# Strided heads' values of two head pairs by Strassen's seven half-size products, spread over the chunks of q and k

## The chip, the core and the metric

The kernel runs on one core of one Trainium2 chip. The time is device microseconds of one execution, as the median of several runs. A profiled execution has a span, from its first to its last instruction, and a trace from which all rows below come. The engines are TensorE (PE; PEld is its weight load), VectorE (DVE), ScalarE (ACT), GpSimd (POOL) and SyncE (SP), which here only issues DMAs, as POOL mostly does.

## The reference, cut to what matters

Two layers of a decoder trunk on x of 512 tokens by 1024 features. Layer 0 is attention with 24 heads in three groups of eight (window and dilation 128 and 1, 512 and 4, 2048 and 16), layer 1 a gated recurrence; each is followed by a gated FFN with a short convolution, and each half layer sits between two RMS norms. The part that changes is the attention:

```python
qkv = (x @ w_qkv).reshape(B, S, N_GROUPS, 3, HEADS_PER_GROUP, HEAD_DIM)
for g in range(N_GROUPS):
    o, lse = dilated_group_attention(qkv[:, :, g, 0], qkv[:, :, g, 1], qkv[:, :, g, 2],
                                     tbl, WINDOWS[g], DILATIONS[g])
    ...
alpha = jax.nn.softmax(jnp.stack(lses), axis=0)
o = jnp.sum(alpha[..., None] * jnp.stack(outs), axis=0)
return o.reshape(B, S, ATTN_OUT_WIDTH).astype(x.dtype) @ w_o
```

The values of the two dilated groups, `qkv[:, :, 1, 2]` and `qkv[:, :, 2, 2]`, are plain products of the normed x (512 x 1024) with weights (1024 x 2048 in all).

## The kernel before

**Products.** Every large product is made in three passes (`PASSES`, L250): both operands are split into hi and lo parts in fp32r, and hi*hi, hi*lo and lo*hi are added in PSUM. `hT` is the normed x, transposed, as such a pair, [128, 8, 512]: features on the partitions, eight chunks k of 128 features, 512 tokens. A product of 512 columns over eight chunks takes 24 matmuls and fills one of eight PSUM banks.

**Weights.** `plan` lists the weight loads in the order of use, 1 MB each. `load` (L188) puts a DMA on SP's queue into one of three `raw` buffers; `pump` (L165) cuts a raw into two pieces and splits each, two ScalarE copies (hi) and two VectorE subtracts (lo) of 512 columns, into one of eight units (`W_UNITS`). `take` hands a unit to a product, `done` gives it back. All program text is in one hand-written order, and each engine works through its own part of it in that order.

**Ticks.** After each tile of 24 matmuls `tick` (L221) is called. It advances the side work (generators in `sides`, each with a delay in ticks), and pumps one piece, or two if fewer than six units are live. So softmaxes, transposes and weight splits come between the tiles of the large products.

**Attention.** First the local group: per pair of heads (`hp`) a chunk of q and a chunk of k (`feat_tiles`, two tiles each; q is evicted by ScalarE, k by VectorE), and for every second pair `values` for four heads. `local` then makes scores S, softmax, transposes PT and output O of one head and leaves the output `o0` in SBUF. Then the two dilated groups together: per pair four chunks (q and k of either group), then `values` (L605): for each of four tiles of 128 tokens 24 matmuls, with `hT` as the stationary and the weights as the moving operand; the tile goes to DRAM (`vrows`) and returns regrouped by residue (`vp`, `by_residue`). `strided` (L719) handles one head: S for both groups and the softmax with the local group's share at its first step, transposes PT two ticks later, O four ticks after that. The tiles of `values` lie between S and PT, and for the last pair they are the last large product ahead of the output projection.

**Output projection.** `rows_proj` (L401) multiplies the heads' outputs, split by `prep` into A[k] (hi and lo), with w_o, in an order of (token tiles, chunks of two heads), here `SHORT_ORDER` (L40). Heads 6 and 7 are chunk 3. When a token tile has all its chunks, `norms` adds it to x and makes the next `hT`. x stays in SBUF (`x_sb`) throughout; gains are loaded to two buffers.

Of the kernel before, what the change touches and what calls it, by code (L numbers as in the profile page):

```python
# [18 lines left out]
P = 128  # L19
S = 512  # L20
# [21 lines left out]
]  # L42

# [34 lines left out]
def kernel(  # L78
# [59 lines left out]
    x_sb = cp.tile([P, 4, D], F32, tag="x_sb", name="x_sb")  # L138

    def gain(src, layer, eng=nc.gpsimd):  # L140
        g = cp.tile([P, D], F32, tag="gain", name=nm("gain"), bufs=2)
        row = src[layer]
        eng.dma_start(g, bass.AP(tensor=row.tensor, offset=row.offset, ap=[[0, P], [1, D]]))
        return g
# [9 lines left out]

    def parts_of(kind, raw):

        if kind == "feat":
            return [raw[:, :, m * P : (m + 1) * P] for m in range(2)]
        if kind == "value":
            return [raw[:, 2 * i : 2 * i + 2, :] for i in range(2)]  # L160
        if kind == "rows":
            return [raw[:, i : i + 1, :] for i in range(2)]
        return [raw]

    def pump(limit=2):  # L165

        for _ in range(limit):
            i = state["cv"]
            if not pieces and i < state["dma"]:
                pieces.extend((i, j, u) for j, u in enumerate(parts_of(plan[i][0], raws.pop(i))))  # L170
                state["cv"] += 1
            if pieces and state["live"] < W_UNITS:
                i, j, raw = pieces.pop(0)
                hi, lo = (
# [12 lines left out]

    def load():  # L188
        i = state["dma"]
        kind, kd, cols, srcs = plan[i]  # L190
        raw = wp.tile([P, kd, cols], F32, tag="raw", name=nm("raw"), bufs=RAW_BUFS)
        at = 0
        for src, n in srcs:
            if i < 2:
                for k in (0, 2):
                    nc.sync.dma_start(raw[:, k : k + 2, :], src[:, k : k + 2, :])
            else:
                nc.sync.dma_start(raw[:, :, at : at + n] if kind == "value" else raw[:, at : at + n, :], src)
            at += n
        raws[i] = raw  # L200
        state["dma"] += 1
# [44 lines left out]

    def w_rows(w, r0):
# [38 lines left out]
    def prenorm(t, hT, g, wait):  # L286
        xh, gh = halves(x_sb[:, t, :]), halves(g)
# [22 lines left out]
    def first_norm(tiles, g):  # L310
# [5 lines left out]
        for j, t in enumerate(tiles):  # L316
            for i, h in enumerate(halves(x_sb[:, t, :])):
# [19 lines left out]
        for j, t in enumerate(tiles):  # L337
            for i, h in enumerate(halves(x_sb[:, t, :])):
# [5 lines left out]
    def postnorm(t, banks, g, final):  # L344
        xh, gh = halves(x_sb[:, t, :]), halves(g)
# [55 lines left out]
    def rows_proj(nchunks, act, order, post, pre):  # L401
# [6 lines left out]
        def prep(n):  # L408
            for k in seq[:n]:
                if k not in A:  # L410
                    A[k] = act(k)
# [6 lines left out]
    def rows_run(nchunks, A, prep, seq, order, post, pre):  # L418
        post_g = gain(*post)
        pre_g, hT = (gain(*pre), new_hT()) if pre is not None else (None, None)  # L420
# [39 lines left out]
    def act_split(srcs):  # L460
        def f(k):
            hi, lo = gen(F32R, "ahi"), gen(F32R, "alo")
# [91 lines left out]
    def attention(hT, post, pre):  # L554
# [50 lines left out]
        def values(vs, permute, midway=None):  # L605

            if permute:
                vd = dp.tile([S, 512], F32, name=f"vrows{len(vrows)}")
                vrows.append(vd)
# [3 lines left out]
            for t in range(4):  # L613
# [22 lines left out]
                for u in (0, 1) if begin and t == 1 else (t,):  # L636
                    o = gen(s="v")
                    nc.scalar.activation(o, banks[u], AF.Copy)
                    if permute:
                        nc.sync.dma_start(vd[u * P : (u + 1) * P, :], o)  # L640
                    else:
                        vs.append(o)
                if t == 3 and permute:
                    by_residue(vd, vs)
                if midway and t == 1:
                    midway()
                tick()

# [21 lines left out]
        def local(h, hh, q, k, v):  # L670
# [46 lines left out]
            o0.append(o)  # L717

        def strided(h, hh, qks, v):  # L719
            st1 = st1_box[0]  # L720
            mx = small(12)
            Ls = []
            for gi, (q, k) in enumerate(qks):
# [10 lines left out]
                Ls.append(L)  # L734
            M, nM, c0, den, s12 = small(4), small(4), small(4), small(4), small(8)
# [44 lines left out]
            o3 = o0[h].rearrange("p (a c) -> p a c", a=4)  # L780
            nc.vector.tensor_tensor(o3, o3, cn.unsqueeze(2).to_broadcast([P, 4, P]), op=ALU.mult)
            yield 4
# [6 lines left out]
            for a in range(4):  # L789
                c = slice(a * P, (a + 1) * P)  # L790
                nc.tensor.transpose(pt0[:, c], o0[h][:, c], ident)
# [24 lines left out]
        next(build)  # L816
        for hp in range(4):
            q, k = [], []
            if hp % 2 == 0:
                v = []  # L820
                values(v, False)
# [3 lines left out]
            feat_tiles(2, hT, qk_sink(q, k, False))  # L825
# [3 lines left out]
        prep, run = rows_proj(4, act_split(oT), SHORT_ORDER, post, pre)  # L829
        for hp in range(4):  # L830
            qs, ks, v = [], [], []
            feat_tiles(4, hT, qk_sink(qs, ks, True))
            both = [(qs[2 * g : 2 * g + 2], ks[2 * g : 2 * g + 2]) for g in range(2)]
            for hh in range(2):
                side(strided(2 * hp + hh, hh, both, v), 1 + hh)
            last = hp == 3
            values(v, True, (lambda: prep(2)) if last else None)
            if last:
                prep(4)
        return run()  # L840
# [97 lines left out]
    qkv, w_in = attn_w_qkv[0], lru_w_in[0]  # L938
    for hp in range(4):
        if hp % 2 == 0:  # L940
            w_value(qkv, (2 * D + hp * 256, 512))
        for j in range(2):
            w_cols(qkv, j * D + hp * 256)
    for hp in range(4):
        for g, j in ((1, 0), (1, 1), (2, 0), (2, 1)):
            w_cols(qkv, g * 3 * D + j * D + hp * 256)
        w_value(qkv, *((g * 3 * D + 2 * D + hp * 256, 256) for g in (1, 2)))
# [28 lines left out]
    for i in range(2):  # L976
        c = slice(i * 512, (i + 1) * 512)
        nc.sync.dma_start(x_sb[:, 0, c], x[0, 0:P, c])
    g = gain(norm_mix_pre, 0, nc.sync)
    load()  # L980
    for t in range(1, 4):
        nc.sync.dma_start(x_sb[:, t, :], x[0, t * P : (t + 1) * P, :])
# [58 lines left out]
```

## Time and profile before

| | |
|---|---|
| median of 3 runs | 1493.47 us (1491.96 to 1495.49) |
| span of the profiled execution | 1492.5 us |
| mean granted TensorE clock | 0.996 |
| stretch 460 to 520 us: TensorE busy | 59.06 of 60.00 us |
| HBM read, over the span | 150.14 MB |

The time of the profiled execution is shown by its span only; the median of the runs stands 1.0 us above it. Values of the strided heads lie at 229.5 us and three times after it, the last ending near 484 us, where the first matmul of the output projection starts (484.1 us). A group row reads: line, engine, operation, output<-inputs, partitions x elements, count | busy us, mean ns of one | idle us before them and who ended it. A timeline row reads: start, duration, engine, line, operation, count of merged instructions, and in brackets the idle time before it. A wait row reads: who waited <- for whom: us in total, times, longest.

### The profile page before, as it was taken

The page shows a single profiled execution, that of the slowest core. Times are in us where ns is not written, and L with a number is a line of the kernel's source. Part 1 is how long each engine was busy: PE and PEld are TensorE (multiplying, and loading weights), DVE is VectorE, ACT ScalarE, POOL GpSimd, SP SyncE. Part 2 cuts the span into 40 slices and gives each one's busy share as a digit, 9 for nine tenths or more (in the row PEclk, how much of TensorE's full clock was granted, in tenths as well). Part 3 has the DMA queues.
Part 4 walks back from the last instruction along what each step waited for, and adds up shares of the span by engine and source line. Part 5 has one row for each costly group of instructions (what it writes and reads, how often), then busy time and mean ns, then how long its engine had stood idle before and what let it go on. Part 6 is the DMA issues. An engine that isn't in the chain of part 4 may idle for free.

```text
span 1492.5 us, 18131 instructions
## 1 busy us (share of the span) xinstructions
PE 1477.9 (99%) x7097; PEld 1240.6 (83%) x7097; DVE 792.7 (53%) x1611; ACT 630.9 (42%) x1282; POOL 34.1 (2%) x67
## 2 busy tenths in 40 slices
PE   8999999999999999999999999999999999999998
PEld 6788888888888898888888888988798888888886
DVE  6344334343434676555565336877876555565333
ACT  5333334343334554344344334479554334344321
POOL 0130000000000000000000000000000000000000
PEclk9999999999999999999999999999999999999999
DMA  7543122424243324232233231342233332323301
GB/s 229 200 140 122 64 88 93 141 92 141 92 141 113 113 93 138 86 104 94 86 112 114 87 111 43 101 145 81 85 99 113 96 102 89 110 85 115 111 1 57
DMA packets 116278, 157.66 MB, mean 106 GB/s; under 512 B 5135, under 2 KB 97511, under 8 KB 116192
## 3 DMA queue, kind: packets, MB, share of 16 engines
q1 hardware_dynamic: 111296, 145.24, 29.3%
q0 software_dynamic: 4896, 11.26, 2.3%
q8 instruction: 56, 0.92, 0.3%
q14 instruction: 30, 0.25, 0.0%
HBM read 150.14 MB, written 11.05 MB: 108 GB/s over the span
## 4 chain that ended last, share of the span: by engine, by line
PE 88%; ACT 5%; DVE 4%; DMA 2%; issue 1%; SPq 0%; POOL 0%; DVEq 0%; ACTq 0%; POOLq 0%
PE ps L254 52%; PE acc L254 22%; PE v L623 8%; DVE wlo L148 1%; DVE xb L853 1%; ACT whi L147 1%; PE S L729 1%; PE tr L303 1%; PE O L787 1%; PE O L714 1%; DMA raw<-in_attn_w_qkv_dram 1%; DMA toe<-skew 1%; ACT sig L874 1%; PE S L679 1%; PE PT L768 0%
## 5 line engine op out<-in xcount | busy, mean ns | idle before, releaser
L254 PE MATMUL ps<-hT,whi 128*128 128x512 f32 (+1 forms) x2752 | 802.1, 376 | 0.0
L254 PEld LDWEIGHTS ps<-hT,whi 128*128 128x128 f32 x2752 | 502.9, 188 | 92.6 <-ACT qk L600 0.6
L254 PE MATMUL ps<-hT,wlo 128*128 128x512 f32 (+1 forms) x1376 | 515.2, 374 | 0.0
L148 DVE TENSOR_TENSOR wlo<-raw,whi 128x512 fp32r<-128x512 f32 x504 | 322.8, 686 | 272.0 <-ACT whi L147 271.8
L147 ACT ACTIVATE whi<-raw 128x512 fp32r<-128x512 f32 x504 | 285.3, 623 | 141.1 <-PE acc L254 120.9
L254 PEld LDWEIGHTS ps<-hT,wlo 128*128 128x128 f32 x1376 | 259.0, 188 | 46.5
L527 DVE SCALAR_TENSOR_TENSOR u<-ps,cols,u 128x511 f32<-128x511 f32 x192 | 143.8, 749 | 140.6 <-ACT u L523 137.2
L254 PE MATMUL acc<-whi,alo 128*128 128x512 f32 x512 | 199.4, 389 | 1.0 <-DVE alo L148 1.0
L254 PE MATMUL acc<-whi,ahi 128*128 128x512 f32 x512 | 200.0, 391 | 0.0
L254 PE MATMUL acc<-wlo,ahi 128*128 128x512 f32 x512 | 199.2, 389 | 0.0
L523 ACT ACTIVATE u<-ps,cols 128x512 f32<-128x512 f32 x96 | 74.8, 779 | 210.1 <-PE ps L254 210.1
L623 PE MATMUL v<-whi,hT 128*128 128x512 f32 x384 | 125.2, 400 | 0.9 <-ACT hT L307 0.9
L254 PEld LDWEIGHTS acc<-whi,alo 128*128 128x128 f32 x512 | 96.1, 188 | 21.4 <-DVE alo L148 1.4
L254 PEld LDWEIGHTS acc<-whi,ahi 128*128 128x128 f32 x512 | 96.1, 188 | 19.7
L254 PEld LDWEIGHTS acc<-wlo,ahi 128*128 128x128 f32 x512 | 96.1, 188 | 19.6
L623 PEld LDWEIGHTS v<-whi,hT 128*128 128x128 f32 x384 | 73.0, 191 | 16.8 <-ACT hT L307 1.6
L623 PE MATMUL v<-wlo,hT 128*128 128x512 f32 x192 | 75.2, 395 | 0.0
L538 ACT ACTIVATE u<-u 128x512 f32<-128x512 f32 x48 | 30.3, 632 | 80.4 <-DVE u L527 80.4
L666 DVE CUSTOM_DVE_ANT_0 L<-S,toe 128x128 f32<-128x128 f32 (+1 forms) x96 | 25.2, 320 | 52.9 <-DMA toe<-skew 22.2
L600 ACT ACTIVATE qk<-ps 128x512 f32<-128x512 f32 x24 | 14.3, 596 | 88.7 <-PE ps L254 76.9
L602 DVE COPY qk<-ps 128x512 f32<-128x512 f32 x24 | 16.6, 691 | 63.0 <-PE ps L254 63.0
L349 DVE TENSOR_TENSOR post<-acc,gain 128x512 f32<-128x512 f32 x32 | 21.8, 687 | 45.7 <-ACT junk L261 45.7
(166 smaller groups left out, 914.9 us busy)
## 6 DMA issues: line engine op xcount, KB each, us to landing
raw<-in_ffn_w_up_dram SPq DMA_DIRECT2D x48, 1024.0 KB, 5.2
raw<-in_attn_w_qkv_dram SPq DMA_DIRECT2D x26, 1024.0 KB, 5.0
raw<-in_ffn_w_down_dram SPq DMA_DIRECT2D x24, 1024.0 KB, 5.0
raw<-in_attn_w_qkv_dram SPq DMA_DIRECT2D x20, 512.0 KB, 5.6
raw<-in_lru_w_in_dram SPq DMA_DIRECT2D x8, 1024.0 KB, 5.4
skew<-rowv POOLq DMA_DIRECT2D x3, 1536.0 KB, 12.2
vrows<-v SPq DMA_DIRECT2D x16, 256.0 KB, 2.5
vp<-vrows SPq DMA_DIRECT2D x16, 256.0 KB, 3.8
```

The lines of the kernel that those rows point to most:

```text
L147: nc.scalar.activation(hi, raw, AF.Copy)
L148: nc.vector.tensor_tensor(lo, raw, hi.bitcast(F32), op=ALU.subtract)
L254: mm(dst, l[a], r[b], start=start and n == 0, stop=stop and n == 2)
L303: nc.tensor.transpose(ps[:, k * P : (k + 1) * P], xs[i][:, k * P : (k + 1) * P], ident)
L349: nc.vector.tensor_tensor(u[i], banks[i], gh[i], op=ALU.mult)
L523: nc.scalar.activation(u, ps, AF.Identity, scale=cc[:, j : j + 1], bias=cc[:, 48 + j : 49 + j])
L527: nc.vector.scalar_tensor_tensor(u[:, d:], ps[:, : S - d], wc, u[:, d:], op0=ALU.mult, op1=ALU.add)
L538: nc.scalar.activation(u, u, AF.Gelu_apprx_tanh)
L602: nc.vector.tensor_copy(dst, src)
L623: mm(banks[t], hT[a][:, k, t * P : (t + 1) * P], W[b][:, k % 2, :], start=(k, a, b) == (0, 0, 0), stop=(k, a, b) == (KD - 1, 1, 0),)
L666: nc.vector.tensor_tensor_reduce(dst, ps, bias, scale=1.0, scalar=3 * NEG, op0=ALU.add, op1=ALU.max, accum_out=mx)
L679: mm(Sp[a // 2][:, o + lo : o + 256], q[hh][:, a * P : (a + 1) * P], k[hh][:, k0 : (a + 1) * P], start=True, stop=True)
```

## The change

The strided heads' values of two head pairs are made together: two pairs of 512 columns side by side, tokens cut into two halves of 256, features into two halves of 512, so that a product of 2 x 2 by 2 x 2 blocks results. Seven block products (in the Winograd form, with sums of hT and of the weights) take the place of eight. Each product is 256 tokens by 512 columns over four chunks of k, in two PSUM banks. The seven are six steps (the first has two products); the first block's steps stand behind the q and k chunks of local pairs 1 to 3, the second's behind the chunks of strided pairs 0 and 1 named in `VALUE_STEPS`. Sums of weights are made in `added`, from raws that are loaded again where needed; sums of hT by `make`, as side work, into buffers that held x; x is loaded again at the end. Local heads' outputs go to DRAM and back (`ow`). Strided pair 3 has no values behind it: its heads score group 1 ahead of the last two chunks, and the output projection takes `LAST_ORDER`. The lru stage keeps `SHORT_ORDER`.

```diff
+LAST_ORDER = [
+    ([0, 1], [0, 1, 2]), ([2], [0]), ([0], [3]), ([1], [3]), ([3], [0]), ([2, 3], [1]), ([2], [2, 3]), ([3], [2, 3]),
+]
+VALUE_STEPS = [(0, 1), (0, 2), (0, 3), (1, 0), (1, 1), (1, 2)]
...
+    def added(kind, j, raw):
+        if kind == "sum0" and j == 0:
+            total["sum"] = cp.tile([P, 4, 512], F32, tag="gain", name=nm("sum"))
+        h = slice(2 * j, 2 * j + 2)
+        part = total["sum"][:, h, :]
+        for n in range(2):
+            old = total["held"][:, h, :] if kind == "sum0" else part
+            nc.vector.tensor_tensor(part[:, n, :], old[:, n, :], raw[:, n, :], op=ALU.add)
+        return part
...
+            terms_of = {
+                3: [((1, 1), 1), ((0, 1), -1)],
+                2: [((0, 0), 1)],
+                4: [((1, 0), -1)],
+                1: [((0, 1), 1), ((0, 0), -1)],
+            }
+            def make(*names):
+                for name in names:
+                    terms = terms_of[name]
+                    T = tuple(cp.tile([P, 4, 256], F32R, tag="x", name=nm("T"), bufs=4) for _ in range(2))
+                    made[name] = T
+                    for m in range(2):
+                        r = run[m].rearrange("p (k c) -> p k c", k=2)
+                        h = slice(2 * m, 2 * m + 2)
+                        parts = [(cut(*ij, x)[:, h, :].bitcast(F32), sg) for ij, sg in terms for x in range(2)]
+                        if name in (3, 1):
+                            (a, _), (b, _) = parts[:2]
+                            nc.vector.tensor_tensor(r, a, b, op=ALU.add)
+                            parts = parts[2:]
+                        for a, sg in parts:
+                            nc.vector.tensor_tensor(r, r, a, op=ALU.add if sg > 0 else ALU.subtract)
+                        split(T[0][:, h, :], T[1][:, h, :], r)
+                        yield 1
...
+        def product(banks, act):
+            i = chunk()
+            for j in range(2):
+                W = take(i, j)
+                for u in range(2):
+                    for k in range(2):
+                        for n, (a, b) in enumerate(PASSES):
+                            mm(
+                                banks[u],
+                                act(a)[:, 2 * j + k, u * P : (u + 1) * P],
+                                W[b][:, k, :],
...
+                done()
...
+            def steps():
+                q = two()
+                c = [gen(s="c") for _ in range(2)]
+                product(q, block(0, 0))
+                for u in range(2):
+                    nc.scalar.activation(c[u], q[u], AF.Copy)
+                q = two()
+                product(q, block(1, 0))
+                o = [gen(s="v") for _ in range(2)]
+                each(o, c, q, ALU.add)
+                out(0, 0, o)
+                side(make(3, 2))
+                yield
+                chunk()
+                q = two()
+                y = [gen(s="y") for _ in range(2)]
+                product(q, total_of(3))
+                each(y, c, q, ALU.add)
+                side(make(4))
+                yield
+                q = two()
+                product(q, total_of(2))
+                each(y, q, y, ALU.subtract)
+                each(c, q, c, ALU.subtract)
+                side(make(1))
+                yield
...
-            o0.append(o)
+            od = dp.tile([P, 512], F32, name=f"o0d{h}")
+            nc.sync.dma_start(od, o)
+            o0.append(od)
...
+                if ahead and not gi:
+                    yield 1
...
-            yield 4
+            yield 2 if ahead else 4
...
         for hp in range(4):
             qs, ks, v = [], [], []
-            feat_tiles(4, hT, qk_sink(qs, ks, True))
...
+            for j in range(4):
+                if j == 3:
+                    by_residue(vrows[hp], v)
+                if j == 2 and last:
+                    both = [(qs[:2], ks[:2])]
+                    heads = [strided(6 + hh, hh, both, v, True) for hh in range(2)]
+                    for g in heads:
+                        next(g)
+                feat_tiles(1, hT, lambda m, ps: sink(2 * j + m, ps))
+                if (hp, j) in VALUE_STEPS:
+                    step(j)
             if last:
+                both.append((qs[2:], ks[2:]))
                 prep(4)
+                for hh, g in enumerate(heads):
+                    next(g)
+                    side(g, 3 + hh)
+                for t in range(4):
+                    xs_sb[t] = load_x(t)
...
+    def quarters(p0):
+        def q(kind, i, f):
+            return kind, qkv, i, [(g * 3 * D + 2 * D + (p0 + f) * 256, 256) for g in (1, 2)]
+        return [
+            [q("value", 0, 0), q("value", 1, 0)],
+            [q("held", 0, 0), q("sum0", 0, 1)],
+            [q("sum", 1, 1)],
+            [q("sum", 1, 0)],
+            [q("value", 1, 1)],
+            [q("held", 0, 1), q("sum0", 1, 1)],
+        ]
```

The remaining steps 3 to 5 make the products of block (1, 1), of sum 4 and of sum 1 in the same manner: one changes c, one writes two tiles out, the last changes y and c and writes both.

More of the change, by code (lines that the diff above doesn't have):

```diff
@@ L173, in pump @@
                 i, j, raw = pieces.pop(0)
+                if plan[i][0] in ("sum0", "sum"):
+                    raw = added(plan[i][0], j, raw)
                 hi, lo = (
@@ L603, in qk, with values @@
             return o
[L605 to L609, printed above, removed]
+        def values(vs):
             ids = [chunk(), chunk()]
@@ L816, in attention, with step @@
         next(build)
+        def step(n):
+            next(steps)
+            tick()
         for hp in range(4):
@@ L975 @@
     root_table()
[L976 to L979, printed above, removed]
+    xs_sb.append(load_x(0, 2))
+    g = gains((norm_mix_pre, 0), eng=nc.sync)[0]
     load()
     for t in range(1, 4):
[L982 removed]
+        xs_sb.append(load_x(t))
         if t == 1:
```

153 lines of the change are left out of this document (115 added, 38 removed).

## The prediction

> **What bounds the kernel now.** First the page's totals and its chain of work, then the list of waits of TensorE alone.
>
> ```profile
> span 1492.5 us, 18131 instructions
> ...
> PE 1477.9 (99%) x7097; PEld 1240.6 (83%) x7097; DVE 792.7 (53%) x1611; ACT 630.9 (42%) x1282; POOL 34.1 (2%) x67
> ...
> PE 88%; ACT 5%; DVE 4%; DMA 2%; issue 1%; SPq 0%; POOL 0%; DVEq 0%; ACTq 0%; POOLq 0%
> ```
>
> ```profile
> PE acc L254 <- DVE alo L148: 1.0, 1, 1.0
> PE O L787 <- DMA vp<-vrows: 0.9, 1, 0.9
> ...
> PE O L714 <- DVE PT L706: 0.5, 1, 0.5
> ```
>
> TensorE is busy 99% and makes 88% of the chain. Once the values have begun it waits three times in the whole attention, 2.4 us in all. The stage lasts as long as its TensorE instructions, and what another engine does is free until TensorE waits for it. How much room the others have is in the busy times by stretch (stretch, length; PE, PEld, DVE, ACT, POOL; clock, DMA share, GB/s), local heads first, then strided ones:
>
> ```profile
> 62.00:170.00 108.00, 107.51 (x525) 88.83 (x524) 41.33 (x128) 39.52 (x99) 17.21 (x31) 1.00 0.38 126
> ...
> 345.00:460.00 115.00, 115.00 (x575) 97.39 (x574) 42.72 (x112) 37.75 (x90) 2.14 (x4) 1.00 0.33 112
> ```
>
> VectorE is busy 0.38 of either. I price the matmuls removed, then VectorE's new work, then the places where it reaches TensorE.
>
> **What is removed.** The page's groups of the values, and TensorE's timeline around one tile of them:
>
> ```profile
> L623 PE MATMUL v<-whi,hT 128*128 128x512 f32 x384 | 125.2, 400 | 0.9 <-ACT hT L307 0.9
> ...
> L623 PE MATMUL v<-wlo,hT 128*128 128x512 f32 x192 | 75.2, 395 | 0.0
> ```
>
> ```profile
> 380.91 0.39 PE L623 MATMUL v<-whi,hT 128*128 128x512 f32 x1
> ...
> 386.35 1.95 PE L729 MATMUL S<-qk,qk 128*128 128x128 f32 x16
> ```
>
> 576 matmuls are six calls of `values` with 96 each; four are the strided ones. Two of these (192) become seven products of 24 (two banks, four chunks of k, three passes), 168; twice over, 48 matmuls go. One tile of 24 takes 386.35 - 380.91 = 5.44 us, 0.227 each (the means of 400 overlap). Gain: 48 x 0.227 = **10.9 us**. I call 5.44 us a slot: a product or a tile of q or k fills one.
>
> Two of the three waits go too: `vp` is fetched a chunk of q and k earlier (0.9), and ([2], [0]) now lies between the last head and the use of its output (1.0): **1.9 us**.
>
> **VectorE's new work.** Prices, from its timeline, from the page for a PSUM source, and from a split that follows directly on an add (VectorE and ScalarE):
>
> ```profile
> 409.74 2.50 DVE L148 TENSOR_TENSOR wlo<-raw,whi 128x512 fp32r<-128x512 f32 x4
> ```
>
> ```profile
> L349 DVE TENSOR_TENSOR post<-acc,gain 128x512 f32<-128x512 f32 x32 | 21.8, 687 | 45.7 <-ACT junk L261 45.7
> ```
>
> ```profile
> 502.61 1.47 DVE L148 TENSOR_TENSOR alo<-oT,ahi 128x512 fp32r<-128x512 f32 x2
> ```
>
> ```profile
> 502.72 0.63 ACT L147 ACTIVATE ahi<-oT 128x512 fp32r<-128x512 f32 x1 [0.33 <-DVE oT L794]
> ```
>
> Back to back, 512 columns take 0.61 us (0.69 alone, and as much from PSUM). A block of two pairs adds: sums of the activations, 2 halves x (3+2+2+3 adds + 4 splits) = 28; sums of the weights, 4 x 4 = 16; splits of 28 half pieces in place of 16, 12; combinations of the products, 16. That is 72 x 0.61 = 44 us, 88 for both blocks; ScalarE gets 8 + 12 and loses 6 of 8 evictions, 14 x 0.6 = 8 us a block. Each block runs over some 145 us of TensorE (local: 6 chunks 65, products 38, values 22, heads 22), which held about 0.38 x 145 = 55 us of VectorE. 99 of 145 fits on average, so most of it costs nothing; it costs where it bunches, since VectorE takes its work in program order and TensorE's small products wait at its end. A half of a sum with three adds takes 3 x 0.61 + 0.70 for ScalarE's copy + 0.65 = 3.2 us, with two 2.6. A piece of weights takes 1.2, a summed one 2.4.
>
> *Place 1, heads 2 and 3.* Two rows of VectorE each for the scores of a local head and for the feature columns, and the exponentials on ScalarE:
>
> ```profile
> 110.87 0.28 DVE L666 CUSTOM_DVE_ANT_0 L<-S,toe 128x128 f32<-128x128 f32 x1
> ...
> 112.31 0.17 DVE L687 COPY st<-s 128x4 f32<-128x4 f32 x1
> ...
> 115.56 0.17 DVE L494 SCALAR_TENSOR_TENSOR s<-cols 128x8 f32<-128x8 f32 x1
> ...
> 119.02 0.17 DVE L507 TENSOR_SCALAR pad<-c 128x8 f32<-128x8 f32 x1
> ```
>
> ```profile
> 112.44 0.41 ACT L692 ACTIVATE L<-L,s 128x128 f32<-128x128 f32 x1 [1.81 <-DVE s L686]
> ...
> 114.23 0.19 ACT L692 ACTIVATION_READ_ACCUMULATOR L<-L,s 128x1 f32 x1
> ```
>
> From the end of step 1, VectorE's order is: y 1.2; halves of sums 2 and 4, 5.2; pump 3.6; feature columns 119.2 - 115.6, say 4; other halves 5.2; scores of head 2 1.6; then exponentials 2.0. Sum 22.8. TensorE reaches head 2's transposes after three slots, two S of 1.3 and the columns' 0.8: 19.7. **3 us**; 0 if VectorE makes up for it in the slots, 5 if it enters late. Before, the same slots held none of the halves. The first product that needs a sum (step 1) comes earlier: its second half is done some 4.1 us after the tile ahead of it (k 0.7, then 3.2), and TensorE has O of a local head (1.6) and half a product (2.7) to do, 4.3: nothing, 2.5 at most if the pump's pieces stand ahead.
>
> *Place 2, strided heads 0 and 1, behind steps 0 to 2.* VectorE's rows of one head's softmax, and TensorE's two transposes:
>
> ```profile
> 387.44 0.29 DVE L666 CUSTOM_DVE_ANT_0 L<-S,toe 128x128 f32<-128x128 f32 x1 [4.44 <-PE S L729]
> ...
> 394.97 0.17 DVE L758 TENSOR_TENSOR s<-s,res 128x16 f32<-128x16 f32 x1
> ...
> 402.54 1.29 DVE L756 TENSOR_TENSOR L<-L,s 128x512 f32<-128x512 f32 x2
> ```
>
> ```profile
> 400.83 1.03 PE L768 MATMUL PT<-ident,L 128*128 128x128 f32 x8
> ...
> 407.42 1.03 PE L768 MATMUL PT<-ident,L 128*128 128x128 f32 x8
> ```
>
> A softmax holds VectorE 7.6 us; head 1's was done 407.42 - 403.8 = 3.6 us early, so this cover was small. Now I list what each tick gives VectorE, from the end of step 0 of the second block. Pump takes one piece, two where fewer than six units are left; by the plan's order these are:
>
> - step 0: o 1.2, a wait of 1.4 for regroup's matmul and its copy 0.2, pump 1.2 + 2.4: 6.4
> - the two q tiles: a half of sum 3 each, 3.2, and 3.6: 6.8 and 6.8
> - step 1: y 1.2, halves of sums 2 and 4, 5.2, pump 3.6: 10.0
> - the two k tiles: k 0.6, other halves 5.2, pump 2.4: 8.2; k 0.6, pump 1.2: 1.8
> - step 2: y and c 2.4, a half of sum 1 3.2, pump 2.4: 8.0
> - the next pair's q tiles: the other half 3.2, head 0's softmax 7.6, pump 1.2: 12.0; head 1's softmax 7.6
>
> That is 67.6. TensorE up to head 1's transposes: ten slots (eight tiles or products of this list, step 3, one k tile) 54.4, the local heads' rest 2.7, two S 3.4, head 0's transposes 1.2 = 61.7. It must fall 6 behind, at sum 3 (1), at each transpose (2 to 3), and a little for banks held by unread products: **6 us**, 2 to 10. While TensorE waits at the transposes, the next tile of k stands behind them, and its eviction is late in turn; while VectorE waits for ScalarE's copy of a sum, the pump's splits and the k evictions stand behind it. Both are in the list. Strided heads 2 to 5 meet no block and cost nothing, as before.
>
> *Place 3, the end.* The values covered the last softmax; now q and k end. The rows of O for one head on TensorE, and the eviction behind it:
>
> ```profile
> 424.86 1.95 PE L787 MATMUL O<-PT,vp 128*128 128x128 f32 x16
> ...
> 427.00 0.71 PE L254 MATMUL ps<-hT,whi 128*128 128x512 f32 x2
> ```
>
> ```profile
> 500.86 1.11 ACT L793 ACTIVATE oT<-O 128x512 f32<-128x512 f32 x1 [3.44 <-issue]
> ```
>
> VectorE after the last tile: k, then head 5's O (1.8 + 1.1 + 0.7), 3.8; pump 1.2; `prep(4)` 2.5: 7.6. Two softmaxes with half of the scores done, 6.7 each: 21.0, and the first half of L 0.7 sooner, 20.3. TensorE gets to head 7's transposes after O 2.1, S 1.7, four half chunks 10.9, head 6's transposes 1.2: 15.9. **4.4 us**; 2 to 7. A[4] to A[7] then fit behind the chunks.
>
> *At nothing.* SP gets ten more weight loads of 1 MB, 8 writes and 8 reads of `o0`, four of x; the writes wait for VectorE and the loads stand behind them.
>
> ```profile
> SPq L198 <- DVE wlo L148: 370.8, 35, 25.4
> ```
>
> ```profile
> raw<-in_attn_w_qkv_dram SPq DMA_DIRECT2D x26, 1024.0 KB, 5.0
> ```
>
> SP mostly waits for a free buffer, so it has time; five or more units (some 20 us) and two raws lie ahead of TensorE, against 5.0 a load. Without that cover, 5 us a late load: 0 to 5. x lands long before its norm; the POOL queue keeps its order, with the next toeplitz tile requested as soon as a buffer is free.
>
> **Sum.** -10.9 - 1.9 + 3 + 6 + 4.4 = +0.6: span 1493.1. The median of the runs, 1493.47, stands 1.0 above the profiled span: **1494.1 us**. 0.2% (3 us) is about what tells from no change; so this is no change, and its own range is 1491 to 1497.
>
> **Rivals.** *VectorE keeps up (faster).* If the buffers (eight banks, units ahead) take up places 1 and 2, only the end costs: -12.8 + 4.4, 1485; with half of the two places, 1489.5. For it: 0.68 average load, three waits before. Against it: the sums of place 2, by order alone, exceed TensorE's.
>
> *The clock drops behind the new waits (slower).* TensorE's first rows:
>
> ```profile
> 9.18 1.69 PE L303 MATMUL tr<-ident,xs 128*128 128x128 f32 x8 [2.06 <-DVE xs L339]
> 11.76 1.22 PE L623 MATMUL v<-whi,hT 128*128 128x512 f32 x2 [0.89 <-ACT hT L307]
> ...
> 13.63 1.91 PE L623 MATMUL v<-whi,hT 128*128 128x512 f32 x4
> 15.34 1.05 PE L623 MATMUL v<-wlo,hT 128*128 128x512 f32 x2
> 16.19 1.21 PE L623 MATMUL v<-whi,hT 128*128 128x512 f32 x4
> 17.24 0.62 PE L623 MATMUL v<-wlo,hT 128*128 128x512 f32 x2
> ```
>
> After a gap of 2.06, transposes and another gap, four matmuls took 15.34 - 13.63 = 1.71, 0.43 each, and only from 16.19 on 0.26: some 4.4 us at half pace, 2.2 lost. The new waits are just gaps with transposes behind. From about 2 us on it could strike: places 1, 2 (twice) and 3, 8.8 more, 1503. Against it: the start had two gaps and transposes in a row, the new waits one each, and the granted clock in both stretches above is 1.00 in spite of their many transposes. The Trainium skill, "TensorE: Matmul & The Clock Gate", Part 1, has the clock halved after an idle window of about 3.4 us; by that, as an estimate, only waits with their transposes over 3.4 us strike, each for 1.7 us, 1499 for three. The half pace at the start agrees with it; no row here shows such a gap later.
>
> **Chances.** No change 0.36, VectorE keeps up 0.30, slower by the clock or by waits at their upper bounds (5 + 10 + 7 give 1502.7) 0.34. The outer parts of the first case shift a little: faster 0.30, same 0.34, slower 0.36. The range goes from between the two outcomes of VectorE keeping up (1489.5, 1485) to about the upper bounds: 1487 to 1502.
>
> **What would show it.** TensorE 48 matmuls fewer; VectorE 792.7 + 88, about 880 us and 144 instructions more; ScalarE about 647. TensorE's waits: PT for L of heads 0, 1 and 7, PT of head 2, a product for sum 3; `vp` and `alo` gone. Wrong if the waits sum far from 14 us, if TensorE waits for weights (raw or a split), or if the granted clock dips within attention.

## The result, and the profile after

| | before | after |
|---|---|---|
| median of 4 runs | 1493.38 us (1491.96 to 1495.49) | 1507.72 us (1507.35 to 1508.44) |
| ratio | | 1.0095, 95% interval 1.008 to 1.0109 |
| span of the profiled execution | 1492.5 us | 1505.7 us |
| mean granted clock | 0.996 | 0.991 |

The changed kernel is slower by 14 us, outside the predicted range. From the page after, its totals and its chain:

```profile
PE 1476.0 (98%) x7049; PEld 1236.2 (82%) x7049; DVE 882.2 (59%) x1755; ACT 648.9 (43%) x1310; POOL 34.2 (2%) x67
...
PE 81%; DVE 8%; ACT 7%; DMA 3%; issue 1%; SPq 0%; POOL 0%; DVEq 0%; ACTq 0%; POOLq 0%
```

The work is as forecast: 48 matmuls fewer, 144 VectorE instructions and 89.5 us of VectorE more, ScalarE at 648.9. But the chain now runs through VectorE for 8% instead of 4%, and TensorE is busy only 1.9 us less. The list of TensorE's waits says where VectorE came in:

```profile
PE PT L928 <- DVE L L916: 8.2, 2, 5.7
...
PE PT L855 <- ACT v L678: 3.4, 1, 3.4
PE PT L928 <- ACT PT L930: 1.6, 1, 1.6
...
PE acc L294 <- DVE alo L164: 1.4, 2, 1.0
```

L928 is the strided transposes (head 0 at 324 us, 5.7; head 7 at 505 us, 2.5 for the scores and 1.6 for a PSUM bank), L855 those of local head 2 (138 us). These are the prediction's places 2, 3 and 1. The wait at L855 has ScalarE's name, but ScalarE waited for VectorE itself: 4.56 us for a half of a sum, then 2.21 for head 2's scores, with the exponentials, a split and the copy of `v` behind them. Its row at those scores:

```profile
134.56 0.40 ACT L846 ACTIVATE L<-L,s 128x128 f32<-128x128 f32 x1 [2.21 <-DVE s L840]
```

Of the two waits on `alo` (L164), one is 0.3 us at the start of the output projection; the other, 1.0 us, lies in layer 1. Three stretches show the clock too (stretch, length; PE, PEld, DVE, ACT, POOL; clock, DMA share, GB/s), first before, then after:

```profile
120.00:150.00 30.00, 30.00 (x154) 25.42 (x153) 11.62 (x21) 10.87 (x20) 0.00 (x0) 1.00 0.32 106
310.00:340.00 30.00, 30.00 (x160) 25.68 (x159) 14.89 (x69) 15.27 (x51) 2.14 (x4) 1.00 0.30 102
480.00:520.00 40.00, 39.06 (x197) 32.90 (x196) 23.17 (x54) 19.94 (x41) 0.00 (x0) 1.00 0.28 95
```

```profile
120.00:150.00 30.00, 24.68 (x116) 20.17 (x115) 18.21 (x62) 12.98 (x34) 1.10 (x2) 0.89 0.26 87
310.00:340.00 30.00, 24.28 (x114) 20.36 (x113) 22.05 (x79) 16.12 (x53) 2.15 (x4) 0.89 0.32 105
480.00:520.00 40.00, 35.04 (x193) 29.40 (x192) 19.72 (x63) 19.71 (x57) 0.00 (x0) 0.96 0.30 106
```

A mean clock of 0.89 over 30 us is 30 x 0.11 x 2 = 6.6 us at half clock, and 0.96 over 40 us is 3.2. The clock fell at each of the three places, while TensorE still waited there.

For an account, I cut the attention in two at matmuls that stand in every kernel of this study: **stretch A** from the first q tile to the first matmul of the output projection, **stretch B** from there to the first of the FFN. Before, then after:

```profile
40.55:484.13 443.58, 443.09 (x2212) 372.88 (x2211) 174.21 (x531) 164.36 (x424) 28.44 (x51) 1.00 0.36 119
...
484.13:535.54 51.41, 50.48 (x251) 42.38 (x250) 34.49 (x80) 26.94 (x60) 0.00 (x0) 1.00 0.32 108
```

```profile
41.02:489.58 448.56, 437.05 (x2144) 365.70 (x2142) 257.85 (x636) 176.63 (x421) 28.62 (x51) 0.98 0.47 158
...
489.58:548.77 59.19, 54.71 (x269) 45.33 (x269) 39.80 (x119) 31.62 (x89) 0.00 (x0) 0.97 0.18 62
```

A and B are 5.0 and 7.8 us longer, 12.8 of the span's 13.2. TensorE's idle time in them (length less busy) went from 0.5 + 0.9 to 11.5 + 4.5 us. Its busy time fell by only 1.8 us in all, since the half clock stretches matmuls; the last experiment, which has the same instructions at full clock, gives 8.2.

### The profile page after: what moved, and what is told of

It is laid out like the page before. It is cut to its first block, busy times and chain, and to the rows that moved or that the text cites. A ratio compares the mean times of both kernels' runs of the same rounds, so it can differ in the third digit from the quotient of the medians.

```text
span 1505.7 us, 18352 instructions
## 1 busy us (share of the span) xinstructions
PE 1476.0 (98%) x7049; PEld 1236.2 (82%) x7049; DVE 882.2 (59%) x1755; ACT 648.9 (43%) x1310; POOL 34.2 (2%) x67
## 4 chain that ended last, share of the span: by engine, by line
PE 81%; DVE 8%; ACT 7%; DMA 3%; issue 1%; SPq 0%; POOL 0%; DVEq 0%; ACTq 0%; POOLq 0%
PE ps L294 50%; PE acc L294 22%; PE vq L723 3%; DVE wlo L164 2%; DMA raw<-in_attn_w_qkv_dram 2%; PE v L663 2%; ACT whi L163 2%; DVE xb L1042 1%; DVE run L710 1%; PE O L947 1%; PE tr L343 1%; DMA toe<-skew 1%; PE O L868 1%; ACT sig L1063 1%; ACT L L904 1%
## 5 line engine op out<-in xcount | busy, mean ns | idle before, releaser
L164 DVE TENSOR_TENSOR wlo<-raw,whi 128x512 fp32r<-128x512 f32 x496 | 318.0, 687 | 233.8 <-ACT whi L163 233.7
L163 ACT ACTIVATE whi<-raw 128x512 fp32r<-128x512 f32 x496 | 281.5, 623 | 141.2 <-PE acc L294 120.8
L663 PE MATMUL v<-whi,hT 128*128 128x512 f32 x128 | 43.4, 417 | 0.3 <-ACT hT L347 0.3
L301 ACT ACTIVATE junk<-acc 128x512 f32<-128x512 f32 x32 | 19.0, 596 | 54.3 <-PE acc L294 54.3
L723 PE MATMUL vq<-whi,T 128*128 128x512 f32 x128 | 42.0, 399 | 0.0
L820 DVE CUSTOM_DVE_ANT_0 L<-S,toe 128x128 f32<-128x128 f32 (+1 forms) x96 | 25.2, 320 | 27.8 <-DMA toe<-skew 12.8
```

Of the source, the lines that this page charges most:

```text
L163: nc.scalar.activation(hi, raw, AF.Copy)
L164: nc.vector.tensor_tensor(lo, raw, hi.bitcast(F32), op=ALU.subtract)
L301: nc.scalar.activation(junk, h, AF.Square, accum_out=ss[:, i : i + 1])
L663: mm(banks[t], hT[a][:, k, t * P : (t + 1) * P], W[b][:, k % 2, :], start=(k, a, b) == (0, 0, 0), stop=(k, a, b) == (KD - 1, 1, 0),)
L723: mm(banks[u], act(a)[:, 2 * j + k, u * P : (u + 1) * P], W[b][:, k, :], start=(j, k, n) == (0, 0, 0), stop=(j, k, n) == (1, 1, 2),)
L820: nc.vector.tensor_tensor_reduce(dst, ps, bias, scale=1.0, scalar=3 * NEG, op0=ALU.add, op1=ALU.max, accum_out=mx)
```

## The experiments

Every kernel is the changed one with the edit shown, timed beside the kernel before. A and B come from the starts of the same matmuls in its trace. Between kernels whose edits lie elsewhere, A differs by up to 1.7 us and B by up to 1.5, so a cost read from one such difference is no surer than that. The trace of "no sums" is of an execution of 1498.16 us, 2.5 above that kernel's median.

| run | median us | ratio, interval | A | B |
|---|---|---|---|---|
| before | 1493.38 | | 443.6 | 51.4 |
| after | 1507.72 | 1.0095 (1.008 to 1.0109) | 448.6 | 59.2 |
| placing alone | 1501.95 | 1.0053 (1.0038 to 1.0068) | 443.0 | 59.6 |
| no sums | 1495.63 | 1.0011 (1.0001 to 1.002) | 437.6 | 60.7 |
| adds on GpSimd | 1518.35 | 1.0161 (1.0146 to 1.0176) | 459.5 | 59.3 |
| dummy matmuls | 1508.89 | 1.0094 (1.0077 to 1.0112) | 449.8 | 60.7 |
| tail reordered | 1520.03 | 1.0171 (1.0156 to 1.0186) | 448.2 | 66.5 |
| heads 0, 1 later | 1507.34 | 1.0085 (1.007 to 1.01) | 448.4 | 60.3 |
| columns later | 1504.92 | 1.0073 (1.0056 to 1.009) | 443.9 | 59.8 |
| four delays | 1510.83 | 1.0111 (1.0096 to 1.0126) | 439.9 | 66.4 |
| steps earlier | 1500.27 | 1.0038 (1.0025 to 1.0051) | 440.2 | 60.1 |
| softmaxes interleaved | 1503.97 | 1.0062 (1.0048 to 1.0076) | 449.8 | 54.3 |
| three together | 1487.47 | 0.9957 (0.9944 to 0.9969) | 433.7 | 54.3 |
| third bias rows later | 1502.9 | 1.0065 (1.0049 to 1.0082) | 443.0 | 60.7 |

### The placing alone, without the seven products

Plain values, two or none to a step, in the same six places; no sums, no second loads.

```diff
-                q = two()
-                c = [gen(s="c") for _ in range(2)]
-                product(q, block(0, 0))
...
+                for p in range(2):
+                    ids = [chunk(), chunk()]
+                    for t in range(4):
+                        bank = psum("v")
...
+                        if (p, t) not in ((0, 0), (1, 2)):
+                            yield
```

> The strided values without Strassen's scheme: eight plain tiles of 24 matmuls for two pairs, in the same six steps; no sums, no second loads of weights. Theory (VectorE's bunches at places 1 and 2, the uncovered softmax at place 3, and half a clock behind each wait): places 1 and 2 go, place 3 stays at about 7.9, the 10.9 of matmuls come back: 1493.4 - 1.9 + 7.9 = 1499. Rival (moving the values is what costs, at all three places): 1507.7 + 10.9 = 1518. Rival (late weights from ten more loads): about 1494.

1501.95, three us above what was expected. TensorE's waits that answer to those of after:

```profile
PE PT L906 <- DVE L L894: 2.5, 1, 2.5
...
PE PT L906 <- ACT PT L908: 1.2, 1, 1.2
```

Places 1 and 2 are empty (the largest wait left in A is one of 1.1 us) and A is as before (443.0 against 443.6); the whole loss stands in B, 8.2 us. So place 3 belongs to the order (heads 6 and 7 behind the last q and k, and the new output order) and not to the seven products.

### The products without their sums

```diff
-            nc.vector.tensor_tensor(part[:, n, :], old[:, n, :], raw[:, n, :], op=ALU.add)
-        return part
+        return raw
...
-                side(make(3, 2))
...
-                return lambda a: T[name][a]
+                return block(1, 1)
```

> The changed kernel without its sums: neither the sums of hT (28 VectorE and 8 ScalarE instructions a block) nor those of the weights (16) are made, the products take plain blocks instead; all matmuls, all weight loads and all combinations stay. Theory: places 1 and 2 (8.3 and 8.6 us) go, place 3 stays: about 1491, at most 1494. Rival (late weights): no change, 1507. Rival (the values' place alone): 1505 or more.

1495.63, a little above the range expected. Place 2 is gone and place 3 stayed (2.5 + 1.6). But a wait came up that was not foreseen, on small loads for the feature columns. TensorE's row there, with its 4.15 us of idle time:

```profile
121.53 0.34 PE L513 MATMUL cols<-ident,st 64*128 64x64 f32 x1 [4.15 <-DMA st<-in_ffn_conv_b_dram]
```

The half clock came behind it here too (0.89 from 120 to 150 us). A loses 11 us against after even so. So VectorE's sums make place 2 and the waits seen at place 1; and transfers between 85 and 125 us are late in the kernel's DMA traffic, with or without sums.

### The adds on GpSimd

```diff
-            nc.vector.tensor_tensor(part[:, n, :], old[:, n, :], raw[:, n, :], op=ALU.add)
+            nc.gpsimd.tensor_tensor(part[:, n, :], old[:, n, :], raw[:, n, :], op=ALU.add)
...
-                            nc.vector.tensor_tensor(r, r, a, op=ALU.add if sg > 0 else ALU.subtract)
+                            nc.gpsimd.tensor_tensor(r, r, a, op=ALU.add if sg > 0 else ALU.subtract)
```

> The adds of both kinds of sums (36 of the 72 added VectorE instructions a block) run on GpSimd. Theory: VectorE loses 22 us a block, places 1 and 2 shrink by more than half: 1491 to 1498. Rival (GpSimd is too slow for the sums, or toeplitz requests wait behind them): 1507 or more.

The rival held: 1518.35. VectorE's subtracts for the weights from 90 to 345 us (busy, mean ns of one), then two rows of GpSimd's adds, and two of VectorE's that lie wholly beside them:

```profile
L164 DVE TENSOR_TENSOR wlo<-raw,whi 128x512 fp32r<-128x512 f32 x67 | 65.2, 1021 | 14.4 <-ACT whi L163 14.4
```

```profile
289.45 6.84 POOL L710 TENSOR_TENSOR run<-run,hT 128x512 f32<-128x512 f32 x4
...
296.26 3.54 POOL L219 TENSOR_TENSOR sum<-sum,raw 128x512 f32<-128x512 f32 x2
```

```profile
289.97 3.48 DVE L164 TENSOR_TENSOR wlo<-sum,whi 128x512 fp32r<-128x512 f32 x2
...
296.76 1.27 DVE L754 TENSOR_TENSOR y<-c,vq 128x512 f32<-128x512 f32 x2
```

```profile
PE cols L520 <- DMA st<-in_lru_lambda_dram: 9.6, 1, 9.6
```

The subtract that reads two operands from SBUF rose from 687 to 1021 ns on average over the whole stretch; wholly beside GpSimd's adds two of its kind (on a summed piece) took 3.48 us, 1.74 each. The instruction with one operand in PSUM stayed as it was, two in 1.27 us. An add on GpSimd took 6.84 / 4 = 1.71 us there. And GpSimd issues the small loads, which now stood behind its adds: one wait of 9.6 us.

### Dummy matmuls ahead of the waits

22 matmuls with no use of their result ahead of head 0's transposes, 17 ahead of head 7's, so that TensorE doesn't stand still.

```diff
+                for _ in range({0: (22, 0), 7: (11, 6)}.get(h, (0, 0))[gi]):
+                    mm(ps, hT[0][:, 0, :P], hT[0][:, 0, :], start=True, stop=True)
```

> The changed kernel with 22 plain matmuls of 512 columns (5 us) on TensorE ahead of head 0's transposes and 17 (3.9 us) ahead of head 7's, into the bank that the transposes then fill: they lie in the wait and keep TensorE busy. Theory (the half clock behind the waits costs by itself): minus 2.8 at place 2 and minus 1.7 at place 3, 1503. Rival (the clock costs nothing): 1507.7, or more by what the matmuls overlap, up to 1510.

1508.89, no gain. TensorE's timeline at heads 0 and 1:

```profile
319.79 5.15 PE L927 MATMUL PT<-hT 128*128 128x512 f32 x22
326.13 1.23 PE L930 MATMUL PT<-ident,L 128*128 128x128 f32 x8 [1.19 <-DVE L L916]
...
334.90 1.23 PE L930 MATMUL PT<-ident,L 128*128 128x128 f32 x8 [1.85 <-DVE L L916]
```

The clock stays full there (1.00 from 310 to 340 us), and head 1, which waited for nothing in the changed kernel, now waits 1.85. At place 2 VectorE sets the pace of both heads: whether TensorE runs at half clock between them or waits, it comes out at the same time. At place 3 the half clock came again, behind the wait for a bank, 1.6 us long and the only one left there.

### Another order at the tail

```diff
-    ([0, 1], [0, 1, 2]), ([2], [0]), ([0], [3]), ([1], [3]), ([3], [0]), ([2, 3], [1]), ([2], [2, 3]), ([3], [2, 3]),
+    ([0, 1], [0, 1]), ([2], [0, 1]), ([0, 1], [2]), ([2], [2]), ([0], [3]), ([1], [3]), ([3], [0, 1]), ([2], [3]), ([3], [2, 3]),
...
-                    side(g, 3 + hh)
+                    side(g, 4 + 2 * hh)
```

> Only place 3 is changed: the output projection takes chunks 0 and 1 for tiles 0 and 1, then 0 and 1 for tile 2, then chunk 2, and the transposes of heads 6 and 7 come 4 and 6 ticks after their softmax in place of 3 and 4. Theory (TensorE comes to head 7's transposes some 4 us before VectorE is done): 5.4 us more lie ahead of them, both waits there go and the half clock with them, 7 of the 7.9: 1501. Rival (VectorE's two softmaxes in a row are late for whatever comes next, A[4] above all): 1505 to 1508.

A miss: 1520.03, with B at 66.5. The two largest new waits:

```profile
PE ps L294 <- ACT hT L347: 4.7, 1, 4.7
PE acc L294 <- ACT PT L930: 4.2, 1, 4.2
```

The third token tile needed a PSUM bank that the transposes' copies gave back late, and the last tile's norm came too late for the FFN. Delay moved the wait and brought another.

### Heads 0 and 1 with more room between scores and transposes

```diff
-            yield 2
+            yield 4 if h < 2 else 2
...
-            yield 2 if ahead else 4
+            yield 2 if ahead or h < 2 else 4
```

> Only place 2 is changed: the transposes of heads 0 and 1 come four ticks after their scores in place of two, O two ticks after that in place of four. Theory (VectorE's queue is some 9 us behind there, and only the transposes feel it): 8.6 go but for 1: about 1500. Rival (the lag moves on to the next tiles, to k's evictions and banks): 1505 or more.

1507.34, the same time. The 5.7 at the transposes went and a product's banks took its place:

```profile
PE vq L723 <- DVE c L754: 4.0, 1, 4.0
```

VectorE's list is what is late at place 2. A consumer moved back only lets the next one find it so.

### The feature columns later

39 ticks later, away from place 1.

```diff
             nc.gpsimd.dma_start(res2, c_res)
-            yield 1
+            yield 40
```

> Only place 1 is changed: the feature columns (VectorE 4 us, TensorE's small transposes, their loads) come 39 ticks later, behind the blocks. Theory (VectorE's order at place 1 is what TensorE waits for): 4 us of VectorE less ahead of head 2's scores, the 8.3 fall to 3 or 4: 1503. Rival (a raw of weights that lands late there, not the order, makes place 1): 1506 or more.

1504.92; A falls by 4.6. From 120 to 150 us the clock is full and TensorE idle for 1.2 us instead of 5.3, although ScalarE still waits for the weights:

```profile
120.00:150.00 30.00, 28.81 (x146) 23.74 (x146) 18.81 (x45) 15.72 (x39) 1.08 (x2) 1.00 0.39 124
```

```profile
ACT whi L163 <- DMA raw<-in_attn_w_qkv_dram: 4.6, 1, 4.6
```

Late weights alone cost TensorE little; late weights and the columns' work together did. The columns met a wait of 1.3 in their new place.

### Four delays at once

The three edits just shown, with the local heads 2 and 3 transposed one tick later:

```diff
-            yield 2
+            yield 3 if h in (2, 3) else 2
```

> The three edits together, and the transposes of local heads 2 and 3 one tick later. Theory (three separate places, together 24.8 us over the matmuls): 8.3 + 8.6 + 7 go but for some 3: 1486. Rival (the places are one lag that shows up again behind each edit): 1495 or more.

1510.83. A is down to 439.9 and B up to 66.4: the tail's order spoils what A gains.

### The second block's steps one chunk earlier

```diff
-VALUE_STEPS = [(0, 1), (0, 2), (0, 3), (1, 0), (1, 1), (1, 2)]
+VALUE_STEPS = [(0, 0), (0, 1), (0, 2), (0, 3), (1, 2), (1, 3)]
```

The list is the second block's alone; the first block, behind the local pairs, stays where it was.

> Only the second block's steps move: behind chunks (0,0) to (0,3), (1,2) and (1,3), so that steps 0 to 2 and all sums but one half lie in strided pair 0, one chunk further ahead of the softmaxes of heads 0 and 1. Theory (place 2 is the sum of VectorE's work between step 0 and head 1's softmax; e8 showed that later transposes only hand the lag on to the banks): 6 to 8 of the 8.6 go, since one more chunk of TensorE (11 us) lies in between: 1500 to 1502. Rival (what lags is made anywhere the block lies): 1505 or more.

1500.27, as expected. Place 2's stretch:

```profile
310.00:340.00 30.00, 30.00 (x160) 25.66 (x159) 21.36 (x80) 15.62 (x51) 2.14 (x4) 1.00 0.47 151
```

TensorE is busy throughout, at full clock, while VectorE does nearly as much as before the edit (21.36 us against 22.05). By A, place 2 cost 448.6 - 440.2 = 8.4 us, and it came from where the work stood, not from how much it was.

### The last two softmaxes interleaved

```diff
+            if ahead:
+                yield 1
             nc.vector.tensor_tensor(den, c0, st1[:, 1, h, :], op=ALU.mult)
...
-                for hh, g in enumerate(heads):
-                    next(g)
-                    side(g, 3 + hh)
+                for _ in range(2):
+                    for g in heads:
+                        next(g)
+                for hh, g in enumerate(heads):
+                    side(g, 3 + hh)
```

> Only the last two softmaxes change: VectorE does the scores of heads 6 and 7, then the sums and scalings of both, so that ScalarE's exponentials of one (3.1 us) lie beside VectorE's work of the other. Theory (place 3 is two softmaxes in a row on VectorE, each with 3 us of waiting for ScalarE): head 7 is ready 3 to 4 us sooner, its waits of 2.5 and 1.6 go but for 1, and with them most of the half clock: 1502 to 1504. Rival (banks set place 3, as e5 suggests): 1506 or more.

1503.97, as expected. In the changed kernel VectorE's row of a softmax shows two pauses of 1.4 for ScalarE's exponentials, at 502.45 and 504.00 us, in which the other head stood behind it; the first is:

```profile
502.45 0.16 DVE L909 TENSOR_TENSOR s<-s,s 128x4 f32<-128x4 f32 x1 [1.38 <-ACT L L904]
```

Interleaved, head 7's transposes wait for a bank alone, 0.77 us in place of 2.5 + 1.6, and the clock stays full; B falls by 4.9:

```profile
504.20 0.60 PE L930 MATMUL PT<-ident,L 128*128 128x128 f32 x4
505.57 0.66 PE L930 MATMUL PT<-ident,L 128*128 128x128 f32 x4 [0.77 <-ACT PT L932]
```

### The three together

Steps earlier, softmaxes interleaved, columns 45 ticks later.

> The steps of e10, the softmaxes of e11 and the feature columns of e9 (45 ticks later) together. Theory: 8.3 falls to 3, 8.6 to 1, 7.9 to 4: 1490 to 1492, faster than before by 2 to 4. Rival (the places are one lag): 1497 or more.

1487.47 in five runs, faster than before by 0.3 to 0.6% and below what was expected. Its page, and A and B:

```profile
PE 1470.2 (99%) x7049; PEld 1232.0 (83%) x7049; DVE 881.7 (59%) x1755; ACT 647.8 (44%) x1310; POOL 34.1 (2%) x67
```

```profile
40.92:474.64 433.72, 432.22 (x2145) 361.97 (x2143) 257.55 (x636) 176.05 (x421) 28.52 (x51) 1.00 0.49 163
```

```profile
474.64:528.94 54.30, 53.16 (x268) 44.20 (x269) 39.74 (x119) 31.48 (x89) 0.00 (x0) 1.00 0.20 68
```

VectorE has the same 1755 instructions and the same busy time. What cost the changed kernel its gain was the order of that work.

### The third group's bias rows later

In the changed kernel a write of 1.5 MB (the third group's bias rows, spread in DRAM) runs from 94 us, while weights come in. Here it stands behind the feature columns, which keep their place.

```diff
-            for g in range(3):
+            for g in range(2):
+                row(g)
                 yield 3
+            yield 3
...
             yield from feature_columns()
+            yield 8
...
+            row(2)
```

> The bias rows of the third group, whose 1.5 MB write to DRAM ran from 94 us while the weights were loaded, are made and written after the feature columns instead; nothing else is changed. Theory (at local heads 2 and 3 the late weights are half of the cost): the 1 MB loads between 85 and 120 us land in about 5 to 6 us, ScalarE's wait of 3.9 for a raw goes, VectorE gets to step 1's y about 3.7 earlier, and TensorE's idle time between 120 and 150 us falls from 5.3 to about 1.5, with no half clock there; median 1502 to 1504. Rival (the feature columns on VectorE are enough by themselves): the loads are on time and head 2's transposes still wait 3 us or more; median 1506 to 1508. Local heads 4 and 5 could meet the moved write in their place.

1502.9: the theory held. The weight loads between 80 and 125 us, first in the changed kernel and then here (number, KB each, median us to landing):

```profile
raw<-in_attn_w_qkv_dram SPq DMA_DIRECT2D x4, 1024.0 KB, 8.7
```

```profile
raw<-in_attn_w_qkv_dram SPq DMA_DIRECT2D x4, 1024.0 KB, 5.3
```

ScalarE's wait for a raw is gone, and TensorE's stretch and wait at place 1 are:

```profile
120.00:150.00 30.00, 27.21 (x145) 23.06 (x144) 17.51 (x61) 13.81 (x36) 1.65 (x3) 1.00 0.39 125
```

```profile
PE PT L863 <- ACT v L686: 2.8, 1, 2.8
```

A is 5.5 shorter. With the weights on time place 1 costs 2.8, and here no half clock followed.

## Why the prediction was wrong

The sum of +0.6 had to be 13.2. By its terms, A's and B's idle time and the full-clock busy time of the three together (432.2 + 53.2 = 485.4 against 493.6 before) give:

| term | predicted | measured |
|---|---|---|
| 48 matmuls fewer | -10.9 | -8.2 |
| old waits (before: A's and B's idle) | -1.9 | -1.4 |
| places 1 and 2 | 9 | 16.3 |
| place 3 | 4.4 | 6.0 |

Measured, places 1 and 2 are A's idle 11.5 and 437.1 - 432.2 = 4.8 (the unrounded values) for the half clock; place 3 is B's idle 4.5 and 1.5. The sum is 12.7. Told by kind, the waits at the three places came to 16.0 where the sum had 13.4, the half clock to 6.3 where it had nothing (at place 2 a longer wait would have stood in for it, as the dummy matmuls show), the gain fell 2.7 short, and the old waits 0.5. So two steps failed: the half clock was put at nothing, the largest term of the miss, and the waits were put too short, at place 1 above all (5.3 us of idle time from 120 to 150 us where it had 3).

- **VectorE's new work** was right in size (about 880 against 882.2), and so was its reading: free on average, paid where it bunches. The three places were the right ones. That "VectorE keeps up" fell.
- **Place 1 is the wait that was furthest off**, and it failed under *At nothing*. Its list of 22.8 against 19.7 took the weights as landed. They were not: DMA moved 249 GB/s from 85 to 120 us where it had moved 167, a 1 MB load took 8.7 us where the last experiment has 5.3, and two splits of the pump came 3.7 late. The stretch before and after, and VectorE's row:

```profile
85.00:120.00 35.00, 34.51 (x178) 29.00 (x177) 15.63 (x59) 14.52 (x41) 13.43 (x25) 1.00 0.51 167
```

```profile
85.00:120.00 35.00, 35.00 (x176) 28.64 (x175) 26.85 (x50) 15.01 (x32) 12.44 (x23) 1.00 0.73 249
```

```profile
109.03 1.29 DVE L164 TENSOR_TENSOR wlo<-raw,whi 128x512 fp32r<-128x512 f32 x2 [3.69 <-ACT whi L163]
```

  Five units and two raws ahead did keep TensorE from waiting for a weight, as it was argued; but VectorE waited, and the whole list behind it came late. Place 1, with its half clock, cost 16.3 - 8.4 = 7.9 us. With the weights on time it is 2.8, beside the 3 predicted: the list itself was good. Why no half clock came beside that wait is not shown: shorter ones met it, as told below.
- **Place 2** was 8.4, not 6, within its bounds. From the end of step 0 to head 1's scores VectorE took 333.3 - 263.0 = 70.3 us where the list said 67.6. Its first and last row, and one half of a sum between:

```profile
263.03 0.69 DVE L754 TENSOR_TENSOR v<-c,vq 128x512 f32<-128x512 f32 x1 [0.67 <-PE vq L723]
...
272.76 0.68 DVE L707 TENSOR_TENSOR run<-hT,hT 128x512 f32<-128x512 f32 x1
...
276.21 1.28 DVE L164 TENSOR_TENSOR wlo<-raw,whi 128x512 fp32r<-128x512 f32 x2
...
333.26 0.17 DVE L918 TENSOR_TENSOR s<-s,res 128x16 f32<-128x16 f32 x1
```

  A half with three adds took 276.21 - 272.76 = 3.45 us, not 3.2. The cost did not spread as the step had it: neither sum 3 nor a bank cost anything, head 0's transposes took one wait of 5.7, and the half clock beside it took the rest, in which VectorE caught up with head 1.
- **Place 3** was right as a wait: 2.5 for the scores and 1.6 for a bank make 4.1 against 4.4. The half clock and small waits on A[0] came on top.
- **The clock** stood in the slower case and not in the sum, where it belonged, since it follows from the waits that the sum had. It struck at three places, for (4.8 + 1.5) / 3 = 2.1 us each, beside the 2.2 taken from the start of the kernel. The argument against it (single gaps, transposes at full clock elsewhere) did not hold. That the clock adds to a wait is not so at place 2, where without it the wait was as much longer. The Trainium skill, "TensorE: Matmul & The Clock Gate", Part 1, halves the clock behind an idle window of about 3.4 us. The runs agree with it only in part: single waits of 3.2, 3.4, 4.0, 4.2 and 5.7 us met the half clock, and a single one of 2.8 did not; but two of 2.5 and 1.6 with transposes between them met it, and so did the one wait of 1.6 left at place 3 with dummy matmuls. Nor had TensorE been idle for 3.4 us each time. The clock fell 0.6 us after the wait at place 1 began. The rows show the 3.41 us ahead of that moment, in which TensorE was busy for 1.78, the half clock itself, and then the 3.41 us ahead of the half clock with dummy matmuls, busy for 1.77. So how long a wait is does not decide alone; what else does stays open.

```profile
131.83:135.24 3.41, 1.78 (x8) 0.91 (x6) 2.82 (x13) 1.20 (x4) 0.56 (x1) 1.00 0.00 0
135.24:142.07 6.83, 3.97 (x13) 3.49 (x14) 4.57 (x18) 4.70 (x18) 0.54 (x1) 0.50 0.60 191
```

```profile
505.94:509.35 3.41, 1.77 (x10) 1.06 (x9) 3.20 (x8) 3.40 (x7) 0.00 (x0) 1.00 0.00 0
```

- **The old waits.** The prediction counted three in the attention, but the third, on `alo`, lies in layer 1's output projection, at 1056.57 us before. It stands in the changed kernel as it did, so its 1.0 us could not go. What went is `vp` (0.9) and the 0.5 of a local head's O.

```profile
1056.57 0.50 PE L254 MATMUL acc<-whi,alo 128*128 128x512 f32 x1 [1.00 <-DVE alo L148]
```

- **The gain** came out 2.7 short. Part of it is pace: in the first product on a sum, three matmuls start every (110.06 - 106.56) / 5 = 0.70 us (below), where a tile of before has 5.44 / 8 = 0.68. With 192 such matmuls (four of the seven products, twice) that is, as an estimate, 192 x 0.02 / 3 = 1.3 us. The rest stays open.

```profile
106.56 0.62 PE L723 MATMUL vq<-whi,T 128*128 128x512 f32 x2
...
110.06 0.63 PE L723 MATMUL vq<-whi,T 128*128 128x512 f32 x2
```

So the slower case came about, by both of its ways at once: the clock at three places, and waits beyond the forecast, place 1 even above its bound of 5.

## What to carry to other kernels

When work goes to an engine with room on average, list what that engine does in program order up to each point where the bounding engine needs it, and count a load that lands in busy DMA traffic as part of that list: the bounding engine may have weights in hand while the engine that feeds it has none. A wait past some 3 us on TensorE is to be priced with the half clock beside it, and so are shorter ones that lie close together or beside transposes. Moving the producer earlier (steps, interleaved softmaxes) removed waits here; moving the consumer later only moved them.

## What was not expected of the hardware

- GpSimd's adds slow VectorE's subtracts with both operands in SBUF from 0.69 to some 1.74 us while they run (1.02 on average over 255 us), and leave those with one operand in PSUM as they were. The Trainium skill, "GPSIMD Engine Reference", section 1, names just this contention, for VectorE instructions with two SBUF inputs; the runs agree and give its size. What inside is shared was not tried.
- How long the half clock lasts did not follow how long the wait was. At 5.7 us of waiting (from 322.98 to 329.80) and at 3.4 it was 6.83 us, and 3.41 behind 2.5 + 1.6 in the changed kernel. With the steps earlier it was 6.83, behind the same two waits. The rows are the half clock at place 3 in these two kernels, the changed one first:

```profile
507.30:510.71 3.41, 3.13 (x11) 2.75 (x12) 3.12 (x9) 2.20 (x5) 0.00 (x0) 0.50 0.63 203
```

```profile
497.76:504.59 6.83, 5.22 (x17) 4.29 (x16) 4.45 (x11) 3.70 (x8) 0.00 (x0) 0.50 0.48 156
```
